# A decoder trunk's transposes through memory move from SP's DMA queue to GpSimd's, and the last layer ends in rows of tokens

## The chip, the cores and the metric

The kernel runs on one core of a Trainium2 chip. Times are device microseconds of one execution, from runs of the same program; lower is better. TensorE (PE) multiplies, VectorE (DVE), ScalarE (ACT) and GpSimd (POOL) work on tiles in SBUF, and DMAs are issued by the queue of SyncE (SP), by ACT's or by POOL's.

## What is computed

A trunk of two decoder layers on 256 tokens of 2048 columns, all in float32. Each layer: a norm, one input projection, four groups of attention heads side by side (forgetting, block-sparse, differential, stick-breaking), an output projection, a residual add, a second norm, a gated feed-forward part and a residual add. A last norm ends the trunk. The reference, cut to its frame:

```python
for l in range(DEPTH):
    h = _rmsnorm(x, attn_norm[l])
    z = jnp.einsum('bsd,dc->bsc', h, w_in[l])
    ...
    mixed = jnp.concatenate([_merge(fox), _merge(moba), _merge(diff), _merge(sb)], axis=-1)
    x = x + jnp.einsum('bsc,cd->bsd', mixed, w_out[l])
    h = _rmsnorm(x, ffn_norm[l])
    act = jax.nn.silu(jnp.einsum('bsd,df->bsf', h, w_gate[l])) * jnp.einsum('bsd,df->bsf', h, w_up[l])
    x = x + jnp.einsum('bsf,fd->bsd', act, w_down[l])
return _rmsnorm(x, final_norm)
```

D is 2048, the feed-forward width 5632, a head 128 wide, four heads to a group.

## The kernel before

Weights stream from memory in blocks of 128 x 1024 float32 (512 KB): 783 whole ones in all. `load` (L188) brings a block to `raw` (four buffers) on SP's queue, `split_parts` (L192) makes two parts of it, `hi` by ACT (L199) and `lo` by DVE (L200), three buffers each, and every product is the sum of three matmuls, activations low by weights high, high by low and high by high. `run_ahead` (L226) issues the splits up to two blocks ahead of the block that TensorE is to use, and the loads ahead of those.

Everything else is written as generators in three queues, `evacs`, `background` and `spare`. After each block `tick` (L269) takes one step of each. A `yield` is so a place in the order: a generator with one `yield` fewer puts what follows one block earlier into the order of every engine. The engines then run their own instructions in that order and wait where data isn't there.

x is held as columns by tokens (`x_all`, 16 tiles of 128 columns x 256 tokens). A product gives tokens by 512 columns (two tiles of 128 tokens in PSUM), so its result has to be turned. `turn_steps` (L394) does it: two DVE transposes of 32 x 32 squares into `tr` (L399), a DMA of 512 KB to memory, `mem` (L402), and four DMAs of 128 KB back into `back`, or straight into `q` or `k` (L408). Both kinds stand in SP's queue, between the weight loads. There are 52 turns: 16 of q and k, 8 of the output projections (`add_turned`, L892), 22 of the feed-forward activations (`act_steps`), 6 of the first three quarters of down. Behind a turn `add_turned` adds to x on DVE (L899), makes the halves of the next layer's or norm's input `xh` (L303 on ACT, L304 on DVE) and sums squares on POOL (L299); `act_steps` copies on ACT (L943) and subtracts on DVE (L944).

Down's last 512 columns are made by `product` (L414), in which the weights are the stationary side of the matmul, so that its result needs no turn; a block there is 8 matmuls of 512 and 8 of 256 columns, or 24 of 256 in the last eleven blocks. `final_norm` (L966) sums squares over partitions by matmuls, spreads the factor by a product with a diagonal matrix (`diag_product`, L316) and writes `y_t`, columns by tokens.

`gate_steps` (L547) runs once a layer in `spare`: DVE and POOL sum x times a gate weight in 32 steps (L565, L566 on POOL), and four heads' sums then go through TensorE (`pf`, L575).

Of the kernel before, what the change touches and what calls it, by code (L numbers as in the profile page):

```python
# [11 lines left out]
F32 = mybir.dt.float32  # L12
# [3 lines left out]
ALU = mybir.AluOpType  # L16
# [85 lines left out]
V_FIN = DEPTH * V_LAYER  # L102
V_ALL = V_FIN + 16


def lay_out(inp):
# [15 lines left out]
    for l in range(DEPTH):  # L122
# [9 lines left out]
        for kind, what, nb in plan():  # L132
# [7 lines left out]
            elif kind == "ffn":  # L140
                c = slice(what[1] * GC, what[1] * GC + GC)
                for n, name in enumerate(("w_gate", "w_up")):
                    blocks[at:at + NJ, :, n * GC:n * GC + GC] = inp[name][l][:, c][pd].reshape(NJ, P, GC)
                at += NJ
            elif kind == "down":
                put(inp["w_down"][l], pf, slice(what[1] * GC, what[1] * GC + GC), GC)
            else:
                put(inp["w_down"][l], pf, pd[what[1] * 256:what[1] * 256 + 256], 256)
    vec[:, V_FIN:V_FIN + 16] = inp["final_norm"][pd].reshape(16, P).T
    return {"x_t": x_t, "vec": vec, "w": blocks, "consts": constants()}  # L150
# [7 lines left out]
def plan():  # L158

    out = []  # L160
    for l in range(DEPTH):
# [4 lines left out]
        out += [("down", (l, c), NFC * 2) for c in range(3)]  # L166
        out += [("last", (l, c), NFC) for c in (6, 7)]
# [4 lines left out]
def trunk(ctx: ExitStack, tc: tile.TileContext, x_t, vec, w, consts, y_t):  # L172
# [143 lines left out]
    def diag_product(cols):  # L316

        diag = tp.tile([P, 2, P], F32, name="diag", tag="g", bufs=1)
        for t in range(2):
            V.tensor_scalar(diag[:, t], ident, cols[:, t:t + 1], None, op0=ALU.mult)  # L320
        yield
        pbc = ps.tile([P, 512], F32, name="pbc", tag="at")
        for t in range(2):
            T.matmul(pbc[:, t * P:(t + 1) * P], cst(C_ONE), diag[:, t], start=t == 0, stop=t == 1)
        return pbc

# [67 lines left out]
    def turn_steps(get, back=None):  # L394
# [16 lines left out]
        yield  # L411
        return back.rearrange("p a k n -> p k a n")

    def product(sources, n_b, tags=("mm",), order=None, split_halves=True, done=None):  # L414


        nonlocal block
        outs = [None] * len(tags)
        for n, kb in order or [(n, kb) for kb in range(n_b) for n in range(len(tags))]:
            if kb == 0:  # L420
                outs[n] = [ps.tile([P, 2 * S], F32, name=f"po{c}", tag=tags[n]) for c in range(2)]
            run_ahead(block)
            hi, lo = halves.pop(block)
            for kk in range(4):
                k = kb * 4 + kk
                xk = sources(k)
                for c in range(2):
                    at = kk * 256 + c * P
                    end = k == 4 * n_b - 1
                    if split_halves:  # L430
                        T.matmul(outs[n][c], hi[:, at:at + P], xk, start=k == 0, stop=False)  # L431
                        T.matmul(outs[n][c][:, S:], lo[:, at:at + P], xk[:, :S], start=False, stop=end)  # L432
                    else:
                        o = outs[n][c][:, :S]
                        T.matmul(o, hi[:, at:at + P], xk[:, S:], start=k == 0, stop=False)
                        T.matmul(o, lo[:, at:at + P], xk[:, :S], start=False, stop=False)
                        T.matmul(o, hi[:, at:at + P], xk[:, :S], start=False, stop=end)
            block += 1
            if done and kb == n_b - 1:
                done(n, outs[n])  # L440
            tick()
        return outs
# [431 lines left out]
    def add_to_x(c, po, gain):  # L874


        def use(j):
            if gain is not None:
                halves_of_x(j, gain(j))
            square_sum(j)  # L880
            if gain is None:
                A.activation(xs[j], xs[j], AF.Copy, scale=vecs[:, V_FIN + j:V_FIN + j + 1])

        for i in range(2):
            j = 2 * c + i
            t = tp.tile([P, S], F32, name="xt", tag="sq")
            V.tensor_tensor(t, xs[j], po[i][:, S:], op=ALU.add)
            V.tensor_tensor(xs[j], t, po[i][:, :S], op=ALU.add)
            if i:
                use(j - 1)  # L890
            yield
        use(2 * c + 1)  # L892
        yield

    def add_turned(n, outs, gain):
# [4 lines left out]
        for j in range(4 * n, 4 * n + 4):  # L900
            if gain is not None:
                halves_of_x(j, gain(j))
            square_sum(j)
            if gain is None:
                A.activation(xs[j], xs[j], AF.Copy, scale=vecs[:, V_FIN + j:V_FIN + j + 1])
            if j % 2:
                yield

# [19 lines left out]
    def ffn(l):  # L928
# [24 lines left out]

        evacs.append(norm_steps("mm"))
# [4 lines left out]
        last = l + 1 == DEPTH  # L959
        gain = None if last else lambda j: vcol(l + 1, V_GA + j)  # L960
        for n in range(3):
# [3 lines left out]
            evacs.append(add_turned(n, outs, gain))  # L965
        if last:  # L966
            A.activation(tp.tile([P, 1], F32, name="pre", tag="pre", bufs=1), cst(C_ONE, 1), AF.Sqrt)
        evacs.append(add_to_x(6, product(source, 11)[0], gain))
        if last:
            final_norm(product(source, 11, split_halves=False)[0])  # L970
        else:
            evacs.append(add_to_x(7, product(source, 11)[0], gain))

    def final_norm(po):

        drain(evacs)
        sums = ps.tile([P, 2], F32, name="sums_ps", tag="at")

        def add(sq, first, last):
            for t in range(2):  # L980
                T.matmul(sums[:, t:t + 1], sq[:, t * P:(t + 1) * P], cst(C_ONE, 1), start=first and t == 0,
                         stop=last and t == 1)

        add(state["acc"], True, False)
        for i in range(2):
            j = NJ - 2 + i
            V.tensor_tensor(xs[j], xs[j], po[i][:, :S], op=ALU.add)
            sq = tp.tile([P, S], F32, name="sq", tag="sq")
            A.activation(sq, xs[j], AF.Square)
            add(sq, False, i == 1)  # L990
        v = tp.tile([P, 2], F32, name="v", tag="nv")
        V.tensor_scalar(v, sums, 1.0 / D, EPS, op0=ALU.mult, op1=ALU.add)
        r = tp.tile([P, 2, 2], F32, name="rf", tag="rf", bufs=1)
        A.activation(r[:, 0], v, AF.Sqrt)
        for j in range(NJ - 2, NJ):
            A.activation(xs[j], xs[j], AF.Copy, scale=vecs[:, V_FIN + j:V_FIN + j + 1])
# [4 lines left out]
        pbc = finish(diag_product(r[:, 0]))  # L1001
# [43 lines left out]
```

## Time and profile before

| | us |
|---|---|
| median of 3 runs | 2255.41 (2245.38 to 2255.88) |
| the profiled execution's own time | 2250.89 |
| its span, from first to last instruction | 2249.1 |
| TensorE busy | 2227.5 |
| VectorE, ScalarE, GpSimd busy | 1300.6, 1056.8, 213.8 |

The mean granted TensorE clock is 0.998 of full speed. Busy time of TensorE overlaps: a matmul's row lasts longer than the distance to the next one's start, so its pace is read from starts. In a timeline row stand the start, the duration, the engine, the line, the operation, what it writes and reads, the count of instructions merged into the row, and in brackets how long the engine had been idle before and what ended that.

### The profile page before, as it was taken

Reading aid. Unit: us, or ns where it says so; the run is one execution under the profiler, and the core shown is the slowest. Engines: PE = TensorE matmul, PEld = TensorE weight load, DVE = VectorE, ACT = ScalarE, POOL = GpSimd, SP = SyncE. Lnnn points to the kernel's source line nnn. Section 1 sums busy time; section 2 is a strip of 40 time slices with the busy share of each in tenths; the row PEclk is TensorE's granted clock in tenths of the full one; section 3 lists DMA queues with packets and bytes.
Section 4 is the critical chain, followed back from the end, with each engine's and each line's share of the span. In section 5 each row is a group of like instructions: output and inputs, shape, how many; then the busy total and the mean of one; then the engine's idle time right before and its main releaser. Section 6 shows DMA issues by size and latency. Waiting matters only on the chain.

```text
span 2249.1 us, 27206 instructions
## 1 busy us (share of the span) xinstructions
PE 2227.5 (99%) x10257; PEld 1845.3 (82%) x10257; DVE 1300.6 (58%) x1450; ACT 1056.8 (47%) x1306; POOL 213.8 (10%) x206
## 2 busy tenths in 40 slices
PE   9999999999999999999999999999999999999998
PEld 6888887788888888888888888887888888888887
DVE  6768655655555555455566776566555555554444
ACT  6455644544444444444444555445444444444443
POOL 2019101100000000000000380011000000000001
PEclk9999999999999999999999999999999999999999
DMA  7766566776667667666657566576666766766674
GB/s 267 223 197 208 179 194 199 233 225 219 211 221 224 210 213 230 210 208 208 199 195 235 183 197 200 165 236 223 219 212 222 223 211 214 228 214 206 212 217 131
DMA packets 187491, 473.31 MB, mean 210 GB/s; under 512 B 17248, under 2 KB 71264, under 8 KB 187360
## 3 DMA queue, kind: packets, MB, share of 16 engines
q1 hardware_dynamic: 186928, 471.05, 65.7%
q8 instruction: 80, 1.31, 0.2%
q10 hardware_dynamic: 432, 0.53, 0.1%
q14 instruction: 51, 0.42, 0.0%
HBM read 442.16 MB, written 29.36 MB: 210 GB/s over the span
## 4 chain that ended last, share of the span: by engine, by line
PE 89%; DMA 4%; DVE 3%; ACT 1%; issue 1%; SPq 1%; DVEq 0%; ACTq 0%
PE gate L389 20%; PE up L389 20%; PE po L371 7%; PE po L373 7%; PE po L372 7%; PE in L371 7%; PE in L372 7%; PE in L373 7%; PE po L431 3%; DMA back<-mem 2%; PE po L432 1%; DVE lo L200 1%; DMA mem<-tr 1%; ACT hi L199 1%; DMA raw<-w 1%
## 5 line engine op out<-in xcount | busy, mean ns | idle before, releaser
L200 DVE TENSOR_TENSOR lo<-raw,hi 128x1024 fp32r<-128x1024 f32 (+1 forms) x785 | 962.9, 1229 | 886.5 <-ACT hi L199 886.2
L199 ACT ACTIVATE hi<-raw 128x1024 fp32r<-128x1024 f32 (+1 forms) x785 | 829.9, 1059 | 1078.5 <-PE up L389 494.5
L389 PE MATMUL gate<-hi,xh 128*128 128x512 f32 x1408 | 548.4, 389 | 0.9 <-ACT hi L199 0.9
L389 PE MATMUL up<-hi,xh 128*128 128x512 f32 x1408 | 548.3, 389 | 0.0
L389 PEld LDWEIGHTS gate<-hi,xh 128*128 128x128 f32 x1408 | 264.5, 188 | 56.4 <-ACT hi L199 1.8
L389 PEld LDWEIGHTS up<-hi,xh 128*128 128x128 f32 x1408 | 264.3, 188 | 54.9
L371 PE MATMUL in<-hi,xh 128*128 128x512 f32 x768 | 303.4, 395 | 1.0 <-ACT hi L199 1.0
L372 PE MATMUL in<-lo,xh 128*128 128x512 f32 x768 | 300.0, 391 | 2.1 <-DVE lo L200 2.1
L373 PE MATMUL in<-hi,xh 128*128 128x512 f32 x768 | 299.5, 390 | 0.0
L389 PE MATMUL gate<-lo,xh 128*128 128x512 f32 x704 | 274.6, 390 | 1.1 <-DVE lo L200 1.1
L389 PE MATMUL up<-lo,xh 128*128 128x512 f32 x704 | 274.2, 389 | 0.0
L299 POOL TENSOR_TENSOR acc<-acc,sq 128x256 f32<-128x256 f32 x73 | 67.9, 930 | 1726.0 <-ACT sq L298 1723.2
L371 PE MATMUL po<-hi,act 128*128 128x512 f32 x528 | 205.5, 389 | 0.0
L373 PE MATMUL po<-hi,act 128*128 128x512 f32 x528 | 205.5, 389 | 0.0
L372 PE MATMUL po<-lo,act 128*128 128x512 f32 x528 | 205.5, 389 | 0.0
L372 PEld LDWEIGHTS in<-lo,xh 128*128 128x128 f32 x768 | 144.5, 188 | 33.3 <-DVE lo L200 4.6
L371 PEld LDWEIGHTS in<-hi,xh 128*128 128x128 f32 x768 | 144.4, 188 | 31.1 <-ACT hi L199 2.3
L373 PEld LDWEIGHTS in<-hi,xh 128*128 128x128 f32 x768 | 144.3, 188 | 30.4
L389 PEld LDWEIGHTS gate<-lo,xh 128*128 128x128 f32 x704 | 132.2, 188 | 30.3 <-DVE lo L200 3.2
L389 PEld LDWEIGHTS up<-lo,xh 128*128 128x128 f32 x704 | 132.1, 188 | 27.3
L373 PEld LDWEIGHTS po<-hi,act 128*128 128x128 f32 x528 | 99.1, 188 | 20.7
L372 PEld LDWEIGHTS po<-lo,act 128*128 128x128 f32 x528 | 99.1, 188 | 20.5
(218 smaller groups left out, 1920.7 us busy)
## 6 DMA issues: line engine op xcount, KB each, us to landing
raw<-w SPq DMA_DIRECT2D x783, 512.0 KB, 4.2
mem<-tr SPq DMA_DIRECT2D x52, 512.0 KB, 4.2
back<-mem SPq DMA_DIRECT2D x176, 128.0 KB, 5.2
k<-mem SPq DMA_DIRECT2D x24, 128.0 KB, 5.0
x_all<-x_t SPq DMA_DIRECT2D x7, 256.0 KB, 6.5
q<-mem SPq DMA_DIRECT2D x8, 128.0 KB, 3.9
y_t<-x_all SPq DMA_DIRECT2D x4, 256.0 KB, 3.0
raw<-w SPq DMA_DIRECT2D x2, 256.0 KB, 3.7
```

Of the source, the lines that this page charges most:

```text
L199: A.activation(hi[:, c], raw[:, c], AF.Copy)
L200: V.tensor_tensor(lo[:, c], raw[:, c], hi[:, c].bitcast(F32), op=ALU.subtract)
L299: G.tensor_tensor(state["acc"], state["acc"], sq, op=ALU.add)
L371: T.matmul(outs[t], xlo, wh, start=first, stop=False)
L372: T.matmul(outs[t], xhi, wl, start=False, stop=False)
L373: T.matmul(outs[t], xhi, wh, start=False, stop=last)
L389: T.matmul(outs[n][t], st, wt[:, n * GC:(n + 1) * GC], start=first, stop=last)
L431: T.matmul(outs[n][c], hi[:, at:at + P], xk, start=k == 0, stop=False)
L432: T.matmul(outs[n][c][:, S:], lo[:, at:at + P], xk[:, :S], start=False, stop=end)
```

## The change

Four things change. In `turn_steps` the DMAs to `mem` and back are issued by POOL's queue (`G`) directly one after the other, and the five `yield`s of the function become four, so that what uses a turn stands one block earlier. All of down goes through `rows_block`, with the activations as the stationary side, in four quarters of 512 columns; layer 0's fourth quarter has a turn of its own. In the last layer x itself is turned to tokens by columns while the feed-forward part runs (`row_steps`, four times, five POOL DMAs each), down's results are added without a turn (`last_steps`), and the squares are summed along the columns by ACT. The last norm scales eight pieces of 128 tokens x 512 columns, five on DVE and three on ACT, and writes `y` as tokens by columns; its gain comes in four loads from a new input, `fin`.

```diff
-        nc.sync.dma_start(mem.rearrange("t i r g n -> (i r) t (g n)"), tr)
-        yield
-        yield
+        G.dma_start(mem.rearrange("t i r g n -> (i r) t (g n)"), tr)
         if back is None:
             back = tp.tile([P, 8, 4, 32], F32, name="back", tag="back", bufs=1)
         for g in range(4):
-            nc.sync.dma_start(back[32 * g:32 * g + 32].rearrange("r a k n -> r a (k n)"),
-                              mem[:, :, :, g].rearrange("t i r n -> r (t i) n"))
-        yield
-        yield
+            G.dma_start(back[32 * g:32 * g + 32].rearrange("r a k n -> r a (k n)"),
+                        mem[:, :, :, g].rearrange("t i r n -> r (t i) n"))
+        for _ in range(3):
+            yield
...
+    def row_steps(n):
+        c = tp.tile([P, 8, 4, 32], F32, name="c", tag="back", bufs=1)
+        A.activation(c, x_all[:, 4 * n:4 * n + 4].rearrange("p k (a n) -> p a k n", n=32), AF.Copy)
+        yield
+        tr = tp.tile([P, 8, P], F32, name="trb", tag="tr", bufs=1)
+        for t in range(2):
+            V.transpose(tr[:, 4 * t:4 * t + 4].rearrange("p a n -> p (a n)"),
+                        c[:, 4 * t:4 * t + 4].rearrange("p a k n -> p (a k n)"))
+        yield
+        mem = dr.tile([8, 32, 4, P], F32, name="memb", tag="mem")
+        for g in range(4):
+            G.dma_start(mem[:, :, g].rearrange("a c n -> c a n"), tr[32 * g:32 * g + 32])
+        G.dma_start(row(n), mem.rearrange("(t i) c g n -> (i c) t (g n)", t=2))
+        yield
...
         for c in range(NFC):
             evacs.append(act_steps(c, *gate_up_product(("at", "mm")[c % 2])))
+            if last and 2 <= c < 6:
+                evacs.append(row_steps(c - 2))
...
-        for n in range(3):
+        for n in range(4):
             outs = [ps.tile([P, GC], F32, name=f"po{t}", tag="mm") for t in range(2)]
             for kb in range(NF // 2):
                 rows_block(source, outs, kb, NF // 2)
-            evacs.append(add_turned(n, outs, gain))
...
+            if not last:
+                evacs.append(add_turned(n, outs, lambda j: vcol(l + 1, V_GA + j)))
+            elif n < 3:
+                evacs.append(last_steps(n, outs, ssq, gains[n]))
         if last:
-            A.activation(tp.tile([P, 1], F32, name="pre", tag="pre", bufs=1), cst(C_ONE, 1), AF.Sqrt)
-        evacs.append(add_to_x(6, product(source, 11)[0], gain))
-        if last:
-            final_norm(product(source, 11, split_halves=False)[0])
-        else:
-            evacs.append(add_to_x(7, product(source, 11)[0], gain))
...
+    def last_steps(n, outs, ssq, gain):
+        x = row(n)
+        for t in range(2):
+            V.tensor_tensor(x[:, t], x[:, t], outs[t], op=ALU.add)
+        yield
+        junk = tp.tile([P, 2, GC], F32, name="junk", tag="tr", bufs=1)
+        for t in range(2):
+            A.activation(junk[:, t], x[:, t], AF.Square, accum_out=ssq[:, t, n:n + 1])
+        yield
+        V.tensor_tensor(x, x, gain[:, None, :].to_broadcast([P, 2, GC]), op=ALU.mult)
...
     def final_norm(outs, ssq, gain):
...
+        for n in range(4):
+            x = row(n) if n < 3 else end
+            for t in range(2):
+                to = y[:, t, n * GC:n * GC + GC]
+                if n == 3 and t == 1:
+                    V.scalar_tensor_tensor(end[:, t], row(3)[:, t], r[:, 0, t:t + 1], gain, op0=ALU.mult, op1=ALU.mult)
+                    nc.sync.dma_start(to, x[:, t])
+                elif t == 0 or n == 3:
+                    V.tensor_scalar(x[:, t], x[:, t], r[:, 0, t:t + 1], None, op0=ALU.mult)
+                    nc.sync.dma_start(to, x[:, t])
+                else:
+                    A.activation(x[:, t], x[:, t], AF.Copy, scale=r[:, 0, t:t + 1])
+                    nc.scalar.dma_start(to, x[:, t])
```

How the rows stand now. First DVE, at the last turn of layer 0's output projection (`po` is the projection's result, `lo` the low part of a weight block, `xh` the halves of x). Before:

```order
L399 STREAM_TRANSPOSE tr<-po_3221 128x512
L399 STREAM_TRANSPOSE tr<-po_3222 128x512
L200 TENSOR_TENSOR lo_3514<-raw_3429,hi_3513 128x1024
L200 TENSOR_TENSOR lo_3534<-raw_3460,hi_3533 128x1024
L200 TENSOR_TENSOR lo_3552<-raw_3490,hi_3551 128x1024
L200 TENSOR_TENSOR lo_3575<-raw_3511,hi_3574 128x1024
L200 TENSOR_TENSOR lo_3593<-raw_3531,hi_3592 128x1024
L899 TENSOR_TENSOR x_all<-x_all,back 128x1024
```

And the same place after the change:

```order
L384 STREAM_TRANSPOSE tr<-po_3226 128x512
L384 STREAM_TRANSPOSE tr<-po_3227 128x512
L196 TENSOR_TENSOR lo_3460<-raw_3371,hi_3459 128x1024
L196 TENSOR_TENSOR lo_3485<-raw_3402,hi_3484 128x1024
L196 TENSOR_TENSOR lo_3503<-raw_3436,hi_3502 128x1024
L196 TENSOR_TENSOR lo_3521<-raw_3457,hi_3520 128x1024
L831 TENSOR_TENSOR x_all<-x_all,back 128x1024
```

Four weight blocks' `lo` stand between the transposes and the addition that needs the turn, where five stood.

Second POOL, at the end of layer 0's forget gate (`gt` and `gacc` are the gate's products and sums; the turn is that of fox's q). Before, the last rows of the gate:

```order
L565 TENSOR_SCALAR gt<-x_all,wf 128x256
L566 TENSOR_TENSOR gacc<-gacc,gt 128x256
L565 TENSOR_SCALAR gt<-x_all,wf 128x256
L566 TENSOR_TENSOR gacc<-gacc,gt 128x256
L299 TENSOR_TENSOR acc<-acc,sq 128x256 x30
```

And after the change:

```order
L518 TENSOR_SCALAR gt<-x_all,wf 128x256
L519 TENSOR_TENSOR gacc<-gacc,gt 128x256
L387 DMA mem<-tr 128x2x512
L391 DMA back<-mem 32x8x128 x4
L518 TENSOR_SCALAR gt<-x_all,wf 128x256
L519 TENSOR_TENSOR gacc<-gacc,gt 128x256
L387 DMA mem<-tr 128x2x512
L391 DMA k<-mem 32x8x128 x4
```

The turn of fox's q stands ahead of the gate's last pair, and that of fox's k behind it; before, POOL's queue held no DMA at all.

## Rows read from the trace of the kernel before

**Rows 1.** The page: the span, and busy time of TensorE (us, share, instructions).

```profile
span 2249.1 us, 27206 instructions
...
PE 2227.5 (99%) x10257; PEld 1845.3 (82%) x10257; DVE 1300.6 (58%) x1450; ACT 1056.8 (47%) x1306; POOL 213.8 (10%) x206
```

**Rows 2.** Who waited for what over the run: us in total, times, longest us.

```profile
ACT act L943 <- DMA back<-mem: 12.2, 13, 2.2
DVE x_all L899 <- DMA back<-mem: 12.0, 7, 2.6
...
PE s L657 <- DMA k<-mem: 0.4, 1, 0.4
```

**Rows 3.** Timeline of DVE in the last turn of layer 0's output projection.

```profile
414.40 1.30 DVE L399 STREAM_TRANSPOSE tr<-po 128x512 f32<-128x512 f32 x2
...
423.71 1.23 DVE L200 TENSOR_TENSOR lo<-raw,hi 128x1024 fp32r<-128x1024 f32 x1 [1.49 <-ACT hi L199]
427.30 1.23 DVE L899 TENSOR_TENSOR x_all<-x_all,back 128x1024 f32<-128x1024 f32 x1 [2.36 <-DMA back<-mem]
```

**Rows 4.** Timeline of SP's queue there.

```profile
415.73 0.38 SPq L402 DMA_DIRECT2D mem<-tr  x1
416.84 1.46 SPq L190 DMA_DIRECT2D raw<-w  x2
419.52 1.80 SPq L408 DMA_DIRECT2D back<-mem  x4
```

**Rows 5.** Timeline of TensorE behind that turn.

```profile
427.63 0.39 PE L389 MATMUL up<-hi,xh 128*128 128x512 f32 x1
...
430.35 0.39 PE L389 MATMUL up<-hi,xh 128*128 128x512 f32 x1
431.08 0.50 PE L389 MATMUL gate<-hi,xh 128*128 128x512 f32 x1 [0.34 <-ACT hi L199]
...
432.34 0.50 PE L389 MATMUL gate<-lo,xh 128*128 128x512 f32 x1 [0.53 <-DVE lo L200]
```

**Rows 6.** Waits in layer 0's output projection, 340 to 440 us.

```profile
DVE x_all L899 <- DMA back<-mem: 5.8, 3, 2.5
```

**Rows 7.** The page, DMA issues: count, KB each, median us to landing.

```profile
mem<-tr SPq DMA_DIRECT2D x52, 512.0 KB, 4.2
back<-mem SPq DMA_DIRECT2D x176, 128.0 KB, 5.2
```

**Rows 8.** Timeline of ACT in a feed-forward turn.

```profile
810.83 1.06 ACT L199 ACTIVATE hi<-raw 128x1024 fp32r<-128x1024 f32 x1 [1.66 <-PE up L389]
814.10 0.63 ACT L943 ACTIVATE act<-back 128x512 fp32r<-128x512 f32 x1 [2.21 <-DMA back<-mem]
```

**Rows 9.** Line 565, POOL: duration in ns, least, median and most.

```profile
L565 POOL TENSOR_SCALAR gt<-x_all,wf x60: 923/980/2031, 160.9 to 1344.8; 128x256 f32<-128x256 f32 x60
```

**Rows 10.** Timeline of POOL: the last of layer 0's gate.

```profile
235.13 0.74 POOL L566 TENSOR_TENSOR gacc<-gacc,gt 128x256 f32<-128x256 f32 x1
```

**Rows 11.** Timeline of DVE: the transposes of fox's q.

```profile
258.54 1.30 DVE L399 STREAM_TRANSPOSE tr<-z 128x512 f32<-128x512 f32 x2
```

**Rows 12.** Timeline of TensorE: the gate's sums.

```profile
266.90 1.28 PE L575 MATMUL pf<-con,gacc 128*128 128x1 f32 x11
```

**Rows 13.** Timeline of TensorE: first and last starts of the last 22 blocks.

```profile
2172.61 0.39 PE L431 MATMUL po<-act,hi 128*128 128x512 f32 x1
...
2203.69 0.28 PE L435 MATMUL po<-act,hi 128*128 128x256 f32 x1
...
2235.25 0.28 PE L437 MATMUL po<-act,hi 128*128 128x256 f32 x1
```

**Rows 14.** Busy time by stretch: us and count by engine, PEclk, DMA share, GB/s.

```profile
2243.00:2245.00 2.00, 0.00 (x0) 0.00 (x0) 1.51 (x5) 0.00 (x0) 0.28 (x1) 0.50 1.03 381
```

**Rows 15.** Timeline of all engines in the tail.

```profile
2238.44 0.48 DVE L320 TENSOR_SCALAR diag<-con,rf 128x128 f32<-128x128 f32 x2
...
2240.90 5.46 SPq L1008 DMA_DIRECT2D y_t<-x_all  x8
```

More of the change, by code (lines that the diff above doesn't have):

```diff
@@ L144, in lay_out @@
                 at += NJ
[L145 removed]
+            else:
                 put(inp["w_down"][l], pf, slice(what[1] * GC, what[1] * GC + GC), GC)
[L147 to L150 removed]
+    fin = np.ascontiguousarray(np.broadcast_to(inp["final_norm"], (P, D)))
+    return {"x_t": x_t, "vec": vec, "w": blocks, "consts": constants(), "fin": fin}
 OUT_ORDER = [(c, kb) for c in range(2) for kb in range(6)] + [(c, kb) for c in range(2) for kb in range(6, 8)]
@@ L165, in plan, with trunk @@
         out += [("ffn", (l, c), NJ) for c in range(NFC)]
-        out += [("down", (l, c), NFC * 2) for c in range(3)]
-        out += [("last", (l, c), NFC) for c in (6, 7)]
+        out += [("down", (l, c), NFC * 2) for c in range(4)]
     return out
 @with_exitstack
-def trunk(ctx: ExitStack, tc: tile.TileContext, x_t, vec, w, consts, y_t):
+def trunk(ctx: ExitStack, tc: tile.TileContext, x_t, vec, w, consts, fin, y):
     nc = tc.nc
@@ L407, in turn_steps @@
         for g in range(4):
-            nc.sync.dma_start(back[32 * g:32 * g + 32].rearrange("r a k n -> r a (k n)"),
-                              mem[:, :, :, g].rearrange("t i r n -> r (t i) n"))
-        yield
-        yield
+            G.dma_start(back[32 * g:32 * g + 32].rearrange("r a k n -> r a (k n)"),
+                        mem[:, :, :, g].rearrange("t i r n -> r (t i) n"))
+        for _ in range(3):
+            yield
         return back.rearrange("p a k n -> p k a n")
[L414 to L442, printed above, removed]
     heads = {}
@@ L900, in add_turned, with row @@
         for j in range(4 * n, 4 * n + 4):
-            if gain is not None:
-                halves_of_x(j, gain(j))
+            halves_of_x(j, gain(j))
             square_sum(j)
-            if gain is None:
-                A.activation(xs[j], xs[j], AF.Copy, scale=vecs[:, V_FIN + j:V_FIN + j + 1])
             if j % 2:
                 yield
+    def row(n):
+        return x_all[:, 4 * n:4 * n + 4].rearrange("p k s -> p (k s)").rearrange("p (t c) -> p t c", t=2)
+    def row_steps(n):
[12 more added lines that the diff above has]
+        yield
     def out_projection(l):
@@ L952, in source @@
             return act[k]
+        last = l + 1 == DEPTH
         evacs.append(norm_steps("mm"))
@@ L964, in ffn @@
                 rows_block(source, outs, kb, NF // 2)
-            evacs.append(add_turned(n, outs, gain))
-        if last:
-            A.activation(tp.tile([P, 1], F32, name="pre", tag="pre", bufs=1), cst(C_ONE, 1), AF.Sqrt)
-        evacs.append(add_to_x(6, product(source, 11)[0], gain))
-        if last:
-            final_norm(product(source, 11, split_halves=False)[0])
-        else:
-            evacs.append(add_to_x(7, product(source, 11)[0], gain))
-    def final_norm(po):
-        drain(evacs)
[L977 to L990, printed above, removed]
+                if last and kb == 4:
+                    gains[n] = big.tile([P, GC], F32, name=f"fin{n}", tag=f"xh{n}")
+                    nc.sync.dma_start(gains[n], fin[:, n * GC:n * GC + GC])
@@ L991, in final_norm @@
+    def final_norm(outs, ssq, gain):
+        drain(evacs)
+        x = row(3)
+        junk = tp.tile([P, 2, GC], F32, name="junk", tag="tr", bufs=1)
+        for t in range(2):
+            V.tensor_tensor(x[:, t], x[:, t], outs[t], op=ALU.add)
+            A.activation(junk[:, t], x[:, t], AF.Square, accum_out=ssq[:, t, 3:4])
+        end = tp.tile([P, 2, GC], F32, name="end", tag="g", bufs=1)
+        V.tensor_tensor(end[:, 0], x[:, 0], gain, op=ALU.mult)
         v = tp.tile([P, 2], F32, name="v", tag="nv")
-        V.tensor_scalar(v, sums, 1.0 / D, EPS, op0=ALU.mult, op1=ALU.add)
+        V.tensor_reduce(v, ssq, axis=AX, op=ALU.add)
+        V.tensor_scalar(v, v, 1.0 / D, EPS, op0=ALU.mult, op1=ALU.add)
```

58 lines of the change are left out of this document (10 added, 48 removed).

## The prediction

> **What bounds the kernel now.** First the page: TensorE is busy for 99% of the span [rows 1]. A busy TensorE is not yet one at its pace, so the second view is the timeline of its matmuls: from 427.63 to 430.35 us lie 12 matmuls of 128x512, one weight block, 2.72 us [rows 5]. That is the beat of the whole kernel, and a change pays only if it takes matmul time away, closes gaps between them, or shortens what stands behind the last one. Third, who waits for the turns: DVE waits 12.0 us for them in seven places, ACT 12.2 us in thirteen, TensorE itself 0.4 us once [rows 2]. Fourth, what such a wait costs. In the last turn of layer 0's output projection DVE's place in its own order is free at 424.94 us (423.71 + 1.23), and the addition starts at 427.30, a wait of 2.36 [rows 3]. Behind it the halves of the next block come late, and TensorE takes 1.99 us over three matmul steps (430.35 to 432.34) in place of 0.68: 1.31 us lost [rows 5]. So here about 1.05 us of a wait is free and the rest is TensorE's time. The kernel is bound by TensorE, with small gaps wherever a turn lands late.
>
> **The change, part by part.**
>
> *Down without `product`.* The 44 weight blocks of the last 512 columns (22 a layer) had the weights as the stationary side. Eleven blocks of the split form last from 2172.61 to 2203.69, 31.08 us, eleven of the unsplit form from there to 2235.37 (last start 2235.25 plus one 0.12 step), 31.68 [rows 13]. In the form of `rows_block` eleven blocks are 11 x 2.72 = 29.92. Three split groups and one unsplit one: 3 x 1.16 + 1.76 = **5.2 us gained**.
>
> *The tail.* Up to the scale's first small operations both tails are alike in length: before, the column sums go through TensorE; after, a second addition of 128x512 (half of 1.30, by the transposes [rows 3]), a square (0.63, by the copy of that size [rows 8]) and a reduction. Then the diagonal matrix, its product and the first multiplication go: from 2238.44 to the first output DMA at 2240.90 are 2.46 us [rows 15], for which one 128x512 scaling comes, 0.65. The 2 MB of output stay and run at 381 GB/s either way [rows 14]. **1.8 us gained.**
>
> *Rows of x in the last layer.* Four `row_steps` put one ACT copy, two DVE transposes and five DMAs each between FFN turns. ACT is idle for about 1.66 us of each 2.72 us block there [rows 8], and that hides them: 0. If that cover were gone they would cost about 1.1 us of ACT each, 4 in all.
>
> *The turns, queue.* No row of before shows a DMA issued by POOL. A turn on SP is, by medians, 4.2 us to land `mem`, three issue steps of 0.45, and 5.2 for the last `back` [rows 4, 7]: 10.8, and 11.6 in the turn of [rows 3]. POOL must issue five in a row. Lower bound of an issue: SP's own 0.45 us. Upper: 2.03 us, the longest POOL operation that reads SBUF; the shortest is 0.92 [rows 9]. I take 0.92, the nearest that an undisturbed POOL instruction shows: five times 0.47 more, +2.3. On the other side, SP puts its weight loads ahead of `back` (two from 416.84 [rows 4]), 512 KB at 381 GB/s being 1.4 us each [rows 14]; a queue of its own may pass both, at most -2.8. The middle is that the two cancel, so I leave the chain as long as it is, and keep 8.4 us (cheap issue, loads passed) and 18.7 (2.03 an issue, none passed) as its ends.
>
> *The turns, one step fewer.* The consumer stands one block earlier in every engine's order (four `lo` rows between transposes and addition instead of five). With an equal chain every consumer's wait grows by one block, 2.72 us. What that costs:
>
> - Output projections, eight turns. In layer 0 three of four wait 5.8 us in all [rows 6]; layer 1 repeats it, since seven waits in the run make 12.0 [rows 2]. Today 11.6 - 6 x 1.05 = 5.3 us are lost. After: 11.6 + 6 x 2.72 - 6.3 = 21.6, and for the two that don't wait, if they land 1 us early, 2 x 0.67 = 1.3. **+17.6.**
> - Down, layer 0: three turns without a wait today, 3 x 0.67 = 2.0. The fourth is new: transposes end some 3.8 us into the next product (a split, 2.4, and the two of [rows 3]), the chain, 11.2, ends near 15, the addition and halves near 17.7, and its seventh block, at 16.3, needs them: 1.4. **+3.4.**
> - FFN, 22 turns. The turn at 814.10 waited 2.21 us [rows 8] and TensorE lost nothing. ACT's place is 1.06 us after a block's start; the wait, the copy (0.63), the next `hi` (1.06) and `lo` (1.25) must be done 8.4 us after it, when the third block needs them: 4.4 us free. Thirteen waits of mean 0.94 [rows 2] become 3.7, the longest 4.9. **+0.5.** This slack is the cover; once gone, each us of chain costs 22.
> - Heads. Scores are matmuls that wait for `k` themselves: 0.4 us today in layer 0 [rows 2], 2.72 more, and 1.7 in layer 1, which I take 1 us early as above. The copies on ACT have FFN's slack. **+4.4.**
> - Forget gate. The last POOL pair stands behind fox's q turn. Today POOL ends the gate at 235.9 [rows 10]; two turns ahead now hold it 7.9 us each and make it wait for their transposes, which still fits. Then: transposes end at 259.84 [rows 11], `mem` lands 4.2 later, four issues 3.7, the pair 1.8: 269.5, where TensorE takes the sums at 266.90 [rows 12]. 2.6 a layer, **+5.2.**
>
> Together +31.1 - 7.0 = **+24 us**. The profiled execution took 2250.89 (span 2249.1 [rows 1]), 0.2% under the median of 2255.41; the sum is made on it: **2275 us**.
>
> **Rivals.** A us of chain is worth about 16 us (twelve additions, two scores, two gates), and 22 more a us once it is over 1.7 longer.
>
> *A. POOL's DMAs land sooner.* POOL is idle in nearly all the run, SP's queue is not; with its own queue the chain may be 8.4 us or less. It decides at 24 / 16 = 1.5 us less, 9.7 us: there the time is 2251. At 8.4 only the 7.0 us of gains are left, 2244; another us less also takes back most of today's 5.3 lost, 2239. Against: five issues on an engine that takes 0.92 us for its shortest read of SBUF.
>
> The Trainium skill (DMA: Bandwidth & Descriptors, Anatomy of one DMA — SWDGE (gpsimd) path) fits a DMA of GpSimd's at 2.0 us plus its bytes at 436 GB/s; as an estimate 3.2 us for `mem` and 2.3 for `back`, a chain near 7 and the time of A. The rows show 4.2 and 5.2 on SP under load, and no run here has shown POOL's.
>
> *B. POOL is slowed by DVE.* The same POOL operation takes 0.92 or 2.03 us [rows 9], and DVE works more than half of the time. At 1.4 an issue the chain is 2.4 longer: 16 x 2.4 + 22 x 0.7 = 54 more, 2329. Against: TensorE never waited for POOL.
>
> The Trainium skill (SBUF — State Buffer, SBUF: two separate sides) says that GpSimd is kept from writing a DMA's descriptors while DVE runs one of its two-port operations, and advises the ACT or SP queue instead; by it B holds. The spread of [rows 9] agrees that something holds POOL up; no run here shows it for a DMA.
>
> *C. It cancels.* A chain of 8.4 to 10.3 us gives 2244 to 2262: the turns' loss eats the 7.0 us.
>
> **Chances.** Forecast (chain 10.3 to 12.9) 0.40, B 0.13, C 0.29, A under 8.4 us 0.18. No change can be told within about 0.5%, 11 us; so faster 0.18, same 0.29, slower 0.53. The range goes from A's 2240 to B's 2330, leaving under 0.1 out at either end; the forecast's own is 2262 to 2310.
>
> **What would show it.** Right: waits of DVE and ACT for `back` longer by about 2.7 us each, TensorE gaps of 3 to 5 us behind each output projection turn, a gap ahead of `pf`, no `po` matmul of 256 columns, the first output DMA 1.8 us sooner after the last matmul. Wrong: if the time from transposes to the last `back` landing is under 9.7 us, the waits shrink and A or C holds; if FFN turns open gaps in TensorE, B.

## The result, and the profile after

The changed kernel takes 2331.71 us (median of 4 runs, 2325.56 to 2342.93), the kernel before 2253.03 beside it (4 runs); the ratio is 1.0365, 95% interval 1.034 to 1.0389. By the ratio it is slower by 3.6%; by the medians it is 79 us, where +24 was forecast. The sign was right, the size was not, and the time lies just outside the range.

The first lines of the page after, to set beside [rows 1]:

```profile
span 2329.4 us, 26788 instructions
...
PE 2254.2 (97%) x9977; PEld 1844.2 (79%) x9977; DVE 1302.2 (56%) x1442; ACT 1047.6 (45%) x1296; POOL 373.4 (16%) x459
```

TensorE has 280 matmuls fewer and is yet busy for 27 us longer: its matmuls have become slower, besides waiting more. The mean granted clock is 0.984 of full speed, where it was 0.998. Next, who waited for what over the run, to set beside [rows 2] (us in total, times, longest):

```profile
ACT act L892 <- DMA back<-mem: 106.3, 22, 7.5
DVE x_all L831 <- DMA back<-mem: 47.3, 12, 7.7
...
PE gate L374 <- ACT hi L195: 16.7, 7, 4.5
PE po L356 <- ACT hi L195: 12.9, 5, 5.6
PE pf L528 <- POOL gacc L519: 8.4, 2, 4.9
PE s L610 <- DMA k<-mem: 6.8, 3, 3.4
```

The two waits for `back` were 12.2 and 12.0 us. Every one of the 22 feed-forward turns and 12 additions now waits, and TensorE stands still behind many of them. The place of [rows 3 to 5], the last turn of layer 0's output projection, in the timeline after:

```profile
429.43 1.30 DVE L384 STREAM_TRANSPOSE tr<-po 128x512 f32<-128x512 f32 x2
431.03 0.72 POOL L387 DMA_DIRECT2D mem<-tr  x1 [2.94 <-DVE tr L384]
437.24 1.23 DVE L196 TENSOR_TENSOR lo<-raw,hi 128x1024 fp32r<-128x1024 f32 x1 [1.49 <-ACT hi L195]
437.37 2.33 POOL L391 DMA_DIRECT2D back<-mem  x4 [5.61 <-DMA mem<-tr]
445.01 1.22 DVE L831 TENSOR_TENSOR x_all<-x_all,back 128x1024 f32<-128x1024 f32 x1 [6.55 <-DMA back<-mem]
...
443.88 0.39 PE L374 MATMUL up<-hi,xh 128*128 128x512 f32 x1
448.79 0.80 PE L374 MATMUL gate<-hi,xh 128*128 128x512 f32 x1 [4.52 <-ACT hi L195]
449.38 0.63 PE L374 MATMUL up<-hi,xh 128*128 128x512 f32 x1
```

DVE reaches the addition at 438.47 and waits 6.55 us for the turn. TensorE stands still from 443.88 to 448.79. In between come the halves of x, `xh`, on ACT and DVE, and the next block's split, which stands behind them in ACT's order. And the matmuls behind the gap start 0.59 us apart, a few steps on 0.43, where [rows 5] has 0.23. The same stretch by windows (busy time of PE, PEld, DVE, ACT, POOL with counts, granted clock, DMA share, GB/s):

```profile
440.00:444.00 4.00, 4.00 (x19) 3.19 (x17) 0.00 (x0) 0.00 (x0) 0.00 (x0) 1.00 0.78 205
444.00:448.90 4.90, 0.38 (x3) 0.12 (x1) 2.56 (x4) 2.63 (x6) 1.51 (x2) 0.79 0.00 0
448.90:453.70 4.80, 4.76 (x11) 3.27 (x12) 4.80 (x5) 3.14 (x6) 1.80 (x2) 0.50 0.32 109
453.70:457.00 3.30, 3.30 (x18) 2.81 (x17) 1.61 (x3) 2.58 (x4) 0.00 (x0) 1.00 0.81 261
```

For 4.8 us behind the gap the granted clock is 0.50, the lower of its two levels (1.2 of 2.4 GHz): TensorE is busy all the time, and the row counts 11 matmuls, where the 3.3 us at full clock behind it count 18. Eleven such stretches lie in the run, all behind gaps of TensorE, and none in the kernel before ahead of its tail.

Adding up the distances between matmul starts in the profiled executions gives the account that the experiments below are read by. "Gaps" are distances over 0.6 us less a normal step of 0.227; "clock" is what matmuls in half-clock stretches took beyond that step, from distances of 0.3 us on.

| us | gaps | clock | span |
|---|---|---|---|
| before | 14.3 | 0.1 | 2249.1 |
| after | 71.8 | 20.6 | 2329.4 |

By stage, after less before, the gaps are: output projections with the feed-forward product behind each +23; the rest of the feed-forward parts +10.6; layer 0's down +5.3; attention, the border of the layers included, +20, of which 8.5 are waits for the gate; the tail -1.6.

A turn, from the end of its transposes to the last landing, took a median of 11.5 us before (52 turns) and 12.7 after (50). Its parts, medians before and after: transposes to issue of `mem` 0.03 and 0.30; `mem` to landing 4.18 and 4.04; landing to the first `back` issue 0.02 and 0.58; first to fourth issue 1.36 and 1.75; fourth issue to the last landing 5.11 and 5.52. The 22 feed-forward turns alone went from a mean of 11.4 to 13.1, the longest 15.1. Medians don't add up; the means of these 22 do, and give +1.7: transposes to `mem` +0.3, its landing -0.5, landing to the first `back` +0.4, first to fourth issue +0.4, fourth issue to the last landing +1.1 (4.9 to 6.0). POOL's issues, by tile (ns, least, median, most), and the page's landings, to set beside [rows 7]:

```profile
L391 POOL DMA_DIRECT2D back<-mem x168: 582/585/610, 69.5 to 2090.7; - x168
L387 POOL DMA_DIRECT2D mem<-tr x50: 717/724/865, 65.1 to 2084.9; - x50
```

```profile
mem<-tr POOLq DMA_DIRECT2D x50, 512.0 KB, 4.0
back<-mem POOLq DMA_DIRECT2D x168, 128.0 KB, 4.8
```

On a queue of their own the median landings are 0.2 and 0.4 us sooner. But the page's median for `back` mixes the four of a turn: over all turns the first lands in 4.3 us, where it was 5.0, and the fourth, which the consumer waits for, in 5.5, where it was 5.1. So the chain is longer by POOL's two pauses, by its slower issues and by the landing of the last `back`. Why that one lands later no run here shows.

The gate, layer 0, POOL and TensorE, to set beside [rows 10] and [rows 12]:

```profile
269.58 0.77 POOL L387 DMA_DIRECT2D mem<-tr  x1 [3.15 <-DVE tr L384]
273.83 2.33 POOL L391 DMA_DIRECT2D back<-mem  x4 [3.48 <-DMA mem<-tr]
276.20 0.93 POOL L518 TENSOR_SCALAR gt<-x_all,wf 128x256 f32<-128x256 f32 x1
277.21 0.72 POOL L519 TENSOR_TENSOR gacc<-gacc,gt 128x256 f32<-128x256 f32 x1
...
277.99 1.23 PE L528 MATMUL pf<-con,gacc 128*128 128x1 f32 x5 [3.55 <-POOL gacc L519]
```

The gate's last pair stands behind fox's q turn as forecast, and TensorE waits for it. The tail: the last matmul and the first output DMA.

```profile
2317.44 0.39 PE L358 MATMUL po<-hi,act 128*128 128x512 f32 x1
...
2321.27 0.34 SPq L970 DMA_DIRECT2D y<-x_all  x1
```

3.83 us lie between them, where it was 5.65 ([rows 13] and [rows 15]): the 1.8 us of the forecast.

### The profile page after: what moved, and what is told of

Same layout as the page of the kernel before. It is cut to its first block, busy times and chain, and to the rows that moved or that the text cites. A ratio compares the mean times of both kernels' runs of the same rounds, so it can differ in the third digit from the quotient of the medians.

```text
span 2329.4 us, 26788 instructions
## 1 busy us (share of the span) xinstructions
PE 2254.2 (97%) x9977; PEld 1844.2 (79%) x9977; DVE 1302.2 (56%) x1442; ACT 1047.6 (45%) x1296; POOL 373.4 (16%) x459
## 5 line engine op out<-in xcount | busy, mean ns | idle before, releaser
L196 DVE TENSOR_TENSOR lo<-raw,hi 128x1024 fp32r<-128x1024 f32 (+1 forms) x785 | 963.4, 1231 | 833.4 <-ACT hi L195 832.4
L357 PE MATMUL po<-lo,act 128*128 128x512 f32 x704 | 274.8, 390 | 2.5 <-DVE lo L196 2.5
L356 PE MATMUL po<-hi,act 128*128 128x512 f32 x704 | 274.2, 390 | 2.1 <-ACT hi L195 2.1
L358 PE MATMUL po<-hi,act 128*128 128x512 f32 x704 | 273.9, 389 | 0.0
L387 POOL DMA_DIRECT2D mem<-tr x50 | 36.7, 734 | 1274.6 <-DVE tr L384 1240.7
L374 PEld LDWEIGHTS gate<-lo,xh 128*128 128x128 f32 x704 | 133.3, 189 | 41.3 <-DVE lo L196 14.3
L357 PEld LDWEIGHTS po<-lo,act 128*128 128x128 f32 x704 | 132.2, 188 | 32.2 <-DVE lo L196 5.0
L356 PEld LDWEIGHTS po<-hi,act 128*128 128x128 f32 x704 | 132.2, 188 | 30.7 <-ACT hi L195 3.4
```

The source lines that it names most:

```text
L196: V.tensor_tensor(lo[:, c], raw[:, c], hi[:, c].bitcast(F32), op=ALU.subtract)
L356: T.matmul(outs[t], xlo, wh, start=first, stop=False)
L357: T.matmul(outs[t], xhi, wl, start=False, stop=False)
L358: T.matmul(outs[t], xhi, wh, start=False, stop=last)
L374: T.matmul(outs[n][t], st, wt[:, n * GC:(n + 1) * GC], start=first, stop=last)
L387: G.dma_start(mem.rearrange("t i r g n -> (i r) t (g n)"), tr)
```

## The experiments

"Before" in each is the same kernel before, run on the same chip as that experiment (2250.8 to 2251.0). L numbers are those of the kernel after, which an edit moves by a few.

**Turns back on SP, at the old place; all else as changed.**

```diff
-        G.dma_start(mem.rearrange("t i r g n -> (i r) t (g n)"), tr)
+        nc.sync.dma_start(mem.rearrange("t i r g n -> (i r) t (g n)"), tr)
+        yield
+        yield
...
-            G.dma_start(back[32 * g:32 * g + 32].rearrange("r a k n -> r a (k n)"),
+            nc.sync.dma_start(back[32 * g:32 * g + 32].rearrange("r a k n -> r a (k n)"),
...
-        for _ in range(3):
-            yield
+        yield
+        yield
```

> The changed kernel with turn_steps as before the change: DMAs of the turns on SP's queue, two yields behind mem and two behind back; down, row_steps and the last norm stay as changed. Theory (the turns alone cost the time, the new down and the new end gain 7.0 us): 2244 to 2247 us, waits of DVE and ACT for back near 12 us each as before, granted clock 0.998. Rival (the new down, row_steps or the new end cost something too, some of the 40 us that layer 0's down and layer 1's attention lost): over 2260 us.

2248.62 us, 0.998 of before (0.9967 to 0.9993), 1.6 us over the expected span. The rival is out: the turns are the loss. But only 2.3 us are gained of the 7.0. The terms themselves came out: layer 0's down is 2.0 us shorter, layer 1's 2.9, what follows the last matmul 2.1. Given back are 3.4 us at the border of the layers, where the addition of down's new fourth turn opens a gap of 2.28 us with half clock behind it, and 3.3 in longer gaps at the output projections and half clock behind one of them.

**SP's queue, one block earlier.** As above with one `yield` behind `back` in place of two.

> As the run on SP's queue with the old places, with one yield fewer behind back, so that what uses a turn stands one block earlier, while the DMAs are issued by SP where they were. Theory (the place costs what the prediction priced, a chain longer by 1.4 us on POOL costs the rest, and the granted clock falls to its lower level behind each long gap of TensorE): out projections +17.6, down +3.4, FFN +0.5, heads +4.4 on some 2245, and some 5 us at the lower clock: 2266 to 2278 us. Rival 1 (the queue alone costs the time): within 3 us of the kernel with the old places. Rival 2 (the place alone costs it): 2315 us or more.

2289.99 us, 1.0161 (1.0134 to 1.0189): 12 us above the theory's span and 25 under the second rival. First the waits of the run with the old places, then those of this one:

```profile
ACT act L894 <- DMA back<-mem: 15.3, 15, 2.1
DVE x_all L833 <- DMA back<-mem: 13.0, 6, 3.3
```

```profile
ACT act L893 <- DMA back<-mem: 75.2, 22, 5.0
DVE x_all L832 <- DMA back<-mem: 39.1, 12, 6.1
```

ACT's waits grew by 59.9 us over 22 turns: 2.72 in the mean, a block; singly by 0.8 to 4.8, since landings differ. The gaps of TensorE grew by 27.5 us (16.2 to 43.7), for which the prediction's terms say 25.9, and 11.9 us more went at half clock. The place alone so costs 41 us in a run with no DMA of a turn on POOL.

**POOL's queue, at the old place.** The changed kernel with four `yield`s in place of three at the end of `turn_steps`.

> The changed kernel with one yield more in turn_steps, so that what uses a turn stands where it stood before the change; its DMAs stay on POOL's queue. Theory (place and a chain 1.4 us longer add up): the chain costs 1.4 us in each out projection turn and each score, the gate still stands behind fox's q turn (8.4 us in two places), some lower clock behind the gate's gaps: 2262 to 2278 us. Rival 1 (POOL's queue alone costs the time, the place is free): 2320 us or more. Rival 2 (the place alone, the queue costs nothing): 2244 to 2250 us.

2281.35 us, 1.013 (1.0096 to 1.0163), 3 us over the expected span. The queue alone costs 33 us against the run with SP's queue at that place: 19.7 more in gaps, 12.4 more at half clock. Place and queue together cost 83, a little more than the 41 and 33 apart.

**The gate's sums three blocks later.**

```diff
                 yield
+        for _ in range(3):
+            yield
         state["gate", l] = yield from gate_end_steps(l, acc)
```

> The changed kernel with the gate's sums (pf) taken by TensorE three blocks later; nothing else differs. Theory (TensorE's 8.4 us of waits for gacc are time lost, and so is the lower granted clock in the stretches right behind them, from 276.2 and 1436.7 us on): 10 to 14 us less than the changed kernel, 2317 to 2322, and no lower clock at those two places. Rival 1 (the clock costs nothing, since TensorE waits elsewhere then): 8 us less. Rival 2 (the waits are hidden by other waits behind them): the same time.

2333.33 us, no gain, as the second rival had it. The waits for `gacc` are gone, and the half clock behind them. Step by step against the changed kernel, 6.4 us are gained at layer 0's gate and 7.7 at layer 1's; 1.2 and 6.0 of them are left when the output projections start, since in layer 0 a wait of 3.0 us for k comes that was not there before. What undoes them stands ahead of or far from the edit: one wait for k in layer 0 was 6.6 us here and 3.8 in the changed kernel, and a gap in layer 0's down, with half clock behind it, costs 6.7. Single waits so vary by as much as what was to be seen, and what the gate is worth over the whole run is not settled; it isn't the 10 to 14 us expected.

**POOL's queue, one block later than before the change.** Five `yield`s in place of three at the end of `turn_steps`.

> The changed kernel with two yields more in turn_steps: POOL's queue, and what uses a turn stands one block later than before the change. Theory (POOL's turn is only about 1.4 us longer, so one block of room, 2.72 us, covers it everywhere but at the gate, whose last pair still stands behind fox's q turn, and at the border of the layers): gaps behind the out projections gone, gaps ahead of pf of 3 to 5 us and the lower clock behind them left, 2254 to 2265 us. Rival (POOL's queue costs by itself, through contention that lengthens other transfers): over 2272 us.

2276.46 us, 1.0114 (1.0094 to 1.0134): above the rival's bound, and hardly better than with four. Its rows don't speak for contention: the median turn is 12.7 us, as in the changed kernel, and no wait of DVE for `back` is over 2.5 us any more. But four gaps stand: 5.5, 5.0 and 6.1 us at the last output projection turns and the border of the layers, where TensorE waits for `xh`, and 4.9 ahead of layer 1's `pf`. Later is there no better; the run with one `yield` more in the output projections, below, shows why.

**Two of the four `back`s on SP.**

```diff
         for g in range(4):
-            G.dma_start(back[32 * g:32 * g + 32].rearrange("r a k n -> r a (k n)"),
-                        mem[:, :, :, g].rearrange("t i r n -> r (t i) n"))
-        for _ in range(3):
-            yield
+            if g == 2:
+                yield
+                yield
+            Q = G if g < 2 else nc.sync
+            Q.dma_start(back[32 * g:32 * g + 32].rearrange("r a k n -> r a (k n)"),
+                        mem[:, :, :, g].rearrange("t i r n -> r (t i) n"))
+        yield
```

> The changed kernel with the third and fourth back of each turn issued by SP's queue, two blocks behind the transposes; mem and the first two stay on POOL, the consumer where it is. Theory (the time from issue to issue on POOL is what its queue costs): the last back starts two steps of 0.58 us earlier, the chain is 11.5 us long in place of 12.7, and the time 2294 to 2308 us. Rival (not the issues but the landings cost it): chain and time within 8 us of the changed kernel's 2331.7.

2303.11 us, 1.0226 (1.0206 to 1.0247), as expected. The median turn is 11.9 us long (the profiled execution was the longest of the four, 2318.26). The fourth `back` is issued 1.0 us sooner behind the transposes than in the changed kernel (means) and lands 0.4 later, though SP issues it. Taking two issues off POOL is worth 1.4% by the two ratios: POOL's issues are a good part of what its queue costs. The later landing stays with two of them gone.

**Gaps made on purpose.** In the run with the old places, some `lo` blocks are computed again by DVE; in four of the nine products TensorE multiplies x with itself meanwhile, which is overwritten.

```diff
-            V.tensor_tensor(lo[:, c], raw[:, c], hi[:, c].bitcast(F32), op=ALU.subtract)
+            for _ in range(1 + again.get(b, 0)):
+                V.tensor_tensor(lo[:, c], raw[:, c], hi[:, c].bitcast(F32), op=ALU.subtract)
...
+            for _ in range(fill.get(block, 0)):
+                T.matmul(outs[0][0], xk[:, :P], xk, start=True, stop=True)
...
+        for c, m, f in ((2, 4, 0), (3, 5, 0), (4, 6, 0), (5, 7, 0), (6, 8, 0), (7, 5, 11), (8, 6, 17), (9, 7, 22), (10, 8, 28)):
+            again[block + 16 * c], fill[block + 16 * c] = m, f
```

> The kernel with turns on SP and the old places, in which VectorE computes lo of the first block of nine gate and up products of each layer again 4 to 8 times, so that TensorE waits some 1.3, 2.5, 3.8, 5.0 and 6.2 us for it; in four of the nine (5, 6, 7 and 8 times) TensorE has 11, 17, 22 and 28 matmuls of 128x512 of x with itself to do in that time, into the result that the product then starts anew. Theory (TensorE's own standing still makes the granted clock fall behind it): the half level right behind the unfilled gaps of 3.8 us and more in both layers, behind 2.5 us perhaps, none behind the filled ones, where TensorE loses only the gap. Rival 1 (what is late, a DMA or VectorE, and not TensorE's idleness goes with the clock): the half level behind filled and unfilled alike. Rival 2 (it comes with turns through POOL or long waits of heads and norms only): no half level in the feed-forward part.

The unfilled gaps are 1.9, 3.2, 4.5, 5.7 and 7.0 us in both layers. Behind the last three the clock is at half in both, behind 3.2 us in one layer and not in the other, behind 1.9 in neither. Behind the eight filled ones it never falls. The time, from one run, is 2348.92 us, with 20.1 us of matmul time lost at half clock. Both places with 7 extra subtractions in layer 0, unfilled and then filled, by windows (columns as above):

```profile
634.90:640.50 5.60, 0.30 (x2) 0.00 (x0) 5.46 (x6) 2.10 (x3) 0.00 (x0) 0.84 0.00 0
640.50:645.70 5.20, 5.16 (x12) 4.08 (x13) 3.57 (x4) 0.44 (x1) 0.00 (x0) 0.51 0.74 250
645.70:651.00 5.30, 5.30 (x25) 4.36 (x24) 3.67 (x4) 1.75 (x3) 0.00 (x0) 1.00 0.53 191
...
832.70:838.30 5.60, 5.53 (x25) 4.25 (x23) 5.46 (x5) 2.21 (x3) 0.00 (x0) 1.00 0.00 0
838.30:843.50 5.20, 4.92 (x21) 4.05 (x22) 4.96 (x6) 1.06 (x1) 0.00 (x0) 1.00 0.70 221
```

DVE is as late in the one as in the other (5.46 us busy in both). What differs is that TensorE stood still, and behind that 12 matmuls fit where 21 do. So the lower clock goes with TensorE's own standing still, and not with the lateness of another engine. That it is so for the changed kernel too, where transfers are late, fits all its eleven stretches, which lie behind gaps.

**One block later in the output projections only, on SP.** The run with the old places, with a `yield` ahead of the addition in the turns of `out_projection`.

> The kernel with turns on SP and the old places, with one yield more ahead of the addition in the out projections' turns alone. Theory (the out projection's turns have 1.05 us of room and wait up to 3.2 us; one block later they wait no more): the gaps at 389, 1503 and 1525 us of the run with the old places go, 7.3 us with some 1.5 us of lower clock, 2239 to 2243 us, under both kernels. Rival (the halves of x then come too late for the gate and up product): 2248 us or more.

2254.48 us, 1.0016 (1.0007 to 1.0024): 6 us slower than without, as the rival had it. The gaps at 389, 1503 and 1525 us are gone as expected; two of 4.99 us come, one in each layer. The first, in the timeline:

```profile
431.38 0.39 PE L374 MATMUL up<-hi,xh 128*128 128x512 f32 x1
431.80 1.06 ACT L195 ACTIVATE hi<-raw 128x1024 fp32r<-128x1024 f32 x1 [1.66 <-PE up L374]
432.89 1.23 DVE L196 TENSOR_TENSOR lo<-raw,hi 128x1024 fp32r<-128x1024 f32 x1 [1.49 <-ACT hi L195]
434.03 1.22 DVE L835 TENSOR_TENSOR x_all<-x_all,back 128x1024 f32<-128x1024 f32 x1
...
436.37 0.79 PE L374 MATMUL gate<-hi,xh 128*128 128x512 f32 x1 [4.60 <-DVE xh L300]
```

The addition waits for no DMA (its row has no bracket). TensorE stops 12 blocks of 2.72 us behind the start of the feed-forward part (398.9), and block 12 needs the x that this addition makes. Its place in DVE's order is behind the split of the block two ahead, which itself waits for TensorE to give a buffer free. Four turns are served one after the other, so delays add up at the last: in layer 0 the four additions start 3.4, 4.1, 5.4 and 6.7 us later than without. A turn so has a latest place as well as an earliest.

**A place for each turn, on SP.** Against the run with the old places:

```diff
-    def turn_steps(get, back=None):
+    def turn_steps(get, back=None, later=0):
...
-        yield
-        yield
+        for _ in range(2 + later):
+            yield
...
-                evacs.append(add_turned(n, outs[n], lambda j: vcol(l, V_GF + j)))
+                evacs.append(add_turned(n, outs[n], lambda j: vcol(l, V_GF + j), n == 1))
...
-                evacs.append(add_turned(n, outs, lambda j: vcol(l + 1, V_GA + j)))
+                evacs.append(add_turned(n, outs, lambda j: vcol(l + 1, V_GA + j), -(n == 3)))
```

> The kernel with turns on SP and the old places, with one yield more in the turn of each out projection's second quarter alone (the one that waits 3.0 and 3.2 us in both layers) and one fewer in the turn of down's fourth quarter in layer 0 (whose addition stood so late that the border of the layers has a gap of 2.28 us). Theory (a turn's place has a latest block, the one that needs the halves of x, and an earliest, where the turn lands; both turns now lie between): the gaps at 389 and 1503 us go with 4.8 us, that at 1137 with 2.0, and most of the 2.9 us of lower clock: 2237 to 2241 us, under the kernel before by 0.4 to 0.6%. Rival (turns are served one after the other, so the second quarter's delay moves the fourth's addition behind block 12 of the feed-forward part, as in the run with one yield more in all four): a gap of 5 us there and 2247 us or more.

2242.38 us, 0.996 (0.9947 to 0.9972), 1.4 us above the expected span: faster than the kernel before by 0.4% and than the changed one by 3.9%. Its page:

```profile
span 2238.4 us, 26628 instructions
...
PE 2217.7 (99%) x9977; PEld 1829.5 (82%) x9977; DVE 1303.1 (58%) x1442; ACT 1054.2 (47%) x1296; POOL 209.6 (9%) x209
```

Gaps are 10.5 us in all, none over 1.4, and no stretch ahead of the tail is at half clock. What the new down and the new end gain is now seen: layer 0's down is 2.2 us shorter than in the kernel before, layer 1's 3.0, what follows the last matmul 2.1.

**A place for each turn, on POOL.** The changed kernel with `4 + later` steps, `later` as above, and 1 for heads and feed-forward turns.

> The changed kernel, POOL's queue, with places by turn: two yields more for heads, the feed-forward part and the out projection's second quarter, one more for its other quarters and down's first three, none for down's fourth in layer 0. Theory (what is left of the loss is the place of each turn and the gate behind fox's q): gaps of the out projections and the border under 2.5 us, gaps ahead of pf of 1.4 to 5 us with lower clock behind them: 2256 to 2268 us, no better than SP's queue with its best places. Rival (with room for its turns POOL's queue wins, since SP is freed): under 2245 us.

2266.95 us, 1.0082 (1.0055 to 1.0109), as expected. Of the 79 us lost, 65 so come back by placing alone, with every DMA of a turn still on POOL. That is more than the 41 of the blanket shift, since many turns now stand a block later than before the change, which makes room for the longer chain too. What is left are gaps ahead of `pf` (2.7 and 7.4 us) and at the third output projection turns (2.7 and 4.3, longer than expected), with half clock behind.

**The change to the turns alone.** The kernel before with the changed `turn_steps`.

> The kernel before with the changed turn_steps alone (POOL's queue, one yield fewer); down's last quarter by the weights-stationary product, and the old end. Theory (the turns make the whole loss; the new down and end give 2.3 us by the run on SP's queue, 7.0 by their own terms): 2333 to 2340 us. Rival (row_steps or down's new turns on POOL's queue add to the loss): under 2325 us.

2326.52 us, 1.0335 (1.032 to 1.035): less than expected, and the rival's bound is not reached either. With POOL's early turns the new down and end show no gain, and the intervals of the two ratios overlap. Layer 1's down and the tail are 11 us shorter in the changed kernel, since three turns are gone there, and layer 0's down, with a fourth turn, 4.3 longer. Some 11 us more go in the other stages, most of it in layer 1, where the changed kernel has `row_steps` too; four executions of one kernel differ by 10 to 17 us, so this can't be put down to a cause.

## Why the prediction was wrong in size

**What held.** TensorE bounds, a wait's free part is small at the output projections and about 4.4 us in the feed-forward part, and one `yield` fewer makes each wait a block longer, in the mean. The terms for the place, 25.9 us of lost TensorE time, came to 27.5 on SP, though shared out otherwise, so that the close sum is in part luck: output projections 12.9 (forecast 17.6), down 5.3 (3.4), feed-forward 1.0 (0.5), attention with the border of the layers 8.4 (4.4). The gains of 5.2 and 1.8 came to 4.9 to 5.2 and 1.9 to 2.1; `row_steps` cost nothing that shows on SP's queue.

**Where the 55 us lie** that the forecast missed: 26 are gaps (57.5 where 31.1 stood), 20.6 the clock. The rest, some 8, is not sorted; longer steps under 0.6 us at full clock take 4.6 of it.

**The step that failed: "the middle is that the two cancel, so I leave the chain as long as it is".** It grew by 1.2 us in the median, 1.7 in the feed-forward part. The issues were cheaper than the 0.92 us taken (0.72 and 0.585). What was not in the sum is a pause of 0.3 us between the transposes and `mem`'s issue and of 0.6 between its landing and the first `back`, where SP has 0.03 and 0.02 in the median. And of the 2.8 us at most that a queue of its own might pass, `mem` got 0.1 and the first `back` 0.7, while the last `back`, which ends the chain, lands 0.4 later, 1.1 in the feed-forward part. The Trainium skill (DMA: Bandwidth & Descriptors, Issuing engines are not separate DMA queues) says that DMAs of all issuing engines run on the same 16 DMA engines and interleave, and that another issuing engine saves issue time alone. The rows agree: over the whole chain the landings got no shorter. The ends of the chain were also set from two lengths, 8.4 from 11.2 and 18.7 from 10.8; the forecast doesn't rest on that.

**The price of the chain was also too low.** By the prediction's 16 us for each us the 1.2 would be 19. It was worked out for one length; the turns are spread from 9.5 to 15.1 us (10.0 to 13.5 before), and those beyond the free 4.4 us of the feed-forward part cost 10.6 us there, where 0.5 stood. Between the runs at the same early place, POOL's costs 28.1 us of gaps more than SP's: 8.5 ahead of `pf`, the rest by turns.

**The term that was missing: the clock.** 20.6 of the 79 us are matmuls at the lower clock behind gaps. The kernel before had no gap long enough to show it, except in its tail, where [rows 14] has the clock at 0.50 behind the last matmuls. The Trainium skill (TensorE: Matmul & The Clock Gate, HAM oscillation — how this bites in real kernels) says that a wait for DMA between stretches of matmuls can start the next stretch at the lower clock; by that page a term was to be had, and the run with gaps made on purpose agrees, with waits for DVE in place of a DMA's.

**The gate** was forecast at 5.2 us and TensorE waited 8.4. The run without that wait gained 7.2 us up to the output projections and was no faster as a whole, so the term can't be said to have been right.

**The rivals.** A fell: the chain got longer, not shorter; the 3.2 and 2.3 us estimated beside it for the landings were 4.0 and 4.8. C fell with it. B's 2329 is next to the result, and its sign, gaps of TensorE behind feed-forward turns, came. But it did not come by B's mechanism, so the nearness is luck: 50 `mem` issues took 0.717 to 0.865 us and 168 `back` issues 0.582 to 0.610, none near 1.4, with DVE busy for 56% of the run. The rule of the Trainium skill beside B (SBUF — State Buffer, SBUF: two separate sides), that DVE's two-port operations hold GpSimd's descriptors up, shows in none of them. "By it B holds" also read it too widely: 962 of DVE's 1302 us are the subtractions of L196, with two inputs, which that section names apart from two-port operations. The spread of [rows 9] comes with POOL's own arithmetic only.

## What to carry to other kernels

Where an engine runs in a written order, a consumer of a transfer has an earliest place, where the data lands, and a latest, ahead of the work that needs its result; move each consumer by its own slack, and don't expect a blanket shift to gain: here one block earlier cost 41 us, and one block later, in the output projections alone, 6. Cost a transfer by its whole chain, pauses between a landing and the next issue included, and up to the landing of its last piece; and by the spread of its lengths, not the median. And where an engine has never stood still long, price a new gap at more than its length: here the eleven stretches at half clock added 20.6 us to 57.5 of gaps.

## What the runs showed of the hardware

A DMA issued by POOL took 0.72 us (512 KB) and 0.585 us (128 KB) of issue, with 0.3 and 0.6 us from the event waited for to its start; on SP it was 0.38 and 0.45, with 0.02 to 0.03 (medians). How long a gap the lower clock follows was not the same everywhere. A distance of 2.28 us at the border of the layers was followed by it on SP at the old place, and so was one of 1.88 at an output projection with SP one block earlier. One of 2.29 in layer 0's down in that run, 2.05 and 2.12 in the changed kernel, and 3.21 in one layer of the run with gaps made on purpose were not. All other longer ones were.
